# Weight units in two halves, a deeper last prep, staged mixer weights and four smaller edits in an eight-core decoder block

## The chip, the cores and the metric

The kernel runs on one Trainium2 chip, on all 8 cores at once; each core works alone on 2048 of the 16384 tokens. The metric is the device time of one execution in microseconds (us), taken from the slowest core. The cores are two dies of four. In some executions one die (sometimes both) is granted a lower TensorE clock, and the time is 2 to 18% longer. Such an execution is called slow here; the others are fast. Because many executions were slow on one die only, I also use **die medians**: the median span of the four cores of a die, for those dies on which every core was granted at least 0.98 of full clock. Their intervals are 1.96 standard errors over the dies, so with 5 to 8 dies they are a little too narrow. Several kernels of one job share the chip and the executions of the kernel before.

## The reference, cut to what matters

```python
def swiglu_ffn(h, w_in, w_out):                      # D_MODEL 2048, D_FF 5632
    gate, up = jnp.split(h @ w_in, 2, axis=-1)
    return (jax.nn.silu(gate) * up) @ w_out
# mixer_block: z = h @ w_in + b_in; a pooling branch and a convolution branch
#   conv branch: GLU -> causal depthwise conv (31 taps) -> LayerNorm over channels -> silu -> @ conv_w_proj
#   merged by gates, then @ w_out                                         [cut]
def reference(x, ...):                               # 4 x 4096 tokens, float32
    x = x + 0.5 * swiglu_ffn(rmsnorm(x, ffn1_norm), ffn1_w_in, ffn1_w_out)
    x = x + mixer_block(rmsnorm(x, mix_norm), ...)
    x = x + 0.5 * swiglu_ffn(rmsnorm(x, ffn2_norm), ffn2_w_in, ffn2_w_out)
    return rmsnorm(x, final_norm)
```

## The kernel before

A core keeps its tokens as rows of 128 channels by tokens, and handles them as two halves of about 1024 tokens. The order of stages is the whole plan of the kernel: FFN 1 on the first half (**A**), the mixer's first part on that half, FFN 1 on the second half (**B**), the mixer's second part on the first half and its first part on the second half, FFN 2 on one half (**C**), in which the mixer's last part ("mixer 2b") is inserted after the first unit of in 2, and FFN 2 on the other half (**D**). Each FFN pass has three chunks of the hidden width, each with an input product ("in 0" to "in 2") and an output product ("out 0" to "out 2").

The FFN products use seven products per 2x2 block of weights in place of eight. A weight unit holds four blocks; two of the seven products use a block as it is ("raw"), five use sums of blocks that VectorE makes. One transfer brings the unit, and every reader waits for the whole of it:

```python
    def send(self, key):
        ...
        bufs = self.half[h:h + size]
        if name in self.staged:                       # already stored as f16: SyncE's queue
            self.P.op(SP, lambda e: e.dma_start(out=dst, in_=src), reads=[self.staged[name][idx]], writes=bufs, ...)
        else:                                         # cast f32 -> f16: GpSimd's queue
            self.P.op(POOL, lambda e: e.dma_start(out=dst, in_=src), reads=self.after.get(len(self.units), ()),
                      writes=bufs, ...)

    PRODUCTS = ((("raw", 0), 3), (("raw", 3), 2), (("d", 0), 6), (("rs", 1), 0), (("rs", 0), 1), (("es", 0), 4),
                (("es", 1), 5))

    def make_sums(ws, sm, nk, part):                  # on VectorE
        rb = ws.bufs
        if part == 0:
            vt(c2(L), sm.d[:, 0:L], rq[:, 0, :], rq[:, 3, :], ALU.add, rb, [sm.b[2]])
        ...
```

Three pieces of background work run in between on VectorE, ScalarE and the queues, one small step after each product. `landed(t0, us)` delays the next step until an estimated time after `t0`; it is a pause in the program's order, not a wait on the chip.

```python
    def prep_forms(nm, h, cg, forms, tiles=None):     # last prep: X2 rows -> normalised inputs of D, two rows deep
        ...
        def load(k):
            if k < 8:
                pair_load(nm, h, k, tiles)
                sent[k] = state["pe"]
            if k - 1 in sent:
                landed(sent[k - 1])

        def done(j):                                  # one conv channel block is finished: store it, CC is reused next
            dma(dr["CD"][S, j], CC.t, [CC.b], [b_CD[S][j]], CC.sem)
            ...
                parts = square_add(CC.t, CC.b, g.t[:, 0:TB], g.b) + [lambda: leave(g)]

            def inverses():                           # LayerNorm: 1/std of all tokens, one instruction
                vec(TB * 6 / 960.0, lambda e: e.reciprocal(out=LNT[:], in_=LNT[:]), [b_LNT], [b_LNT])

        def put(j):                                   # second LayerNorm: one row of CN, one buffer for all rows
                act(CNT.t, t, AF.Silu, ...)           # ScalarE writes the row ...
                dma(dr["CN"][:, j, :], CNT.t, [CNT.b], [b_CND[j]], CNT.sem)   # ... and it is stored
```

The first weights wait for row 4 of x, and the second half of x waits for the first weights (`W.after = {0: b_X0[0, 4], ...}` and `ahead = ... W.units[0].bufs`). The mixer's weights (conv_w_proj, w_out) come as f32 with a cast in both mixers.

## Time and profile before

| | kernel before |
|---|---|
| first three executions | 4760.07, 4757.5 us (fast), 5540.49 us (slow) |
| die medians, 34 dies of the first three jobs of experiments | 4742.5 us (95%: +-2.0) |

In a timeline each line is: start, us, engine, line of the source, operation, out<-in, count, and in brackets how long the engine had stood and which engine or transfer ended that. BIG stands for all of the program's large on-chip rows; raw is the buffer of the weight units; CC is the row of one conv channel block, CD and CN are its copies off the chip, before and after the second LayerNorm; MD is what the mixer's last part reads, and X2 what FFN 2 reads. The timeline of core 1 before, around the conv block whose CC buffer is written again:

```profile
1818.68 0.81 DVE L1049 TENSOR_SCALAR BIG<-BIG,CST 128x1024 f32<-128x1024 f32 x1 [5.78 <-DMA CD<-BIG]
...
1823.41 7.08 PE L555 MATMUL PSUM<-BIG 128*128 128x512 bf16 x32 [1.54 <-DVE BIG L477]
...
1836.88 2.75 PE L555 MATMUL PSUM<-BIG,raw 128*128 128x512 bf16 x12 [3.80 <-DVE BIG L477]
```

VectorE stands 5.78 us until the store of CC to CD has landed. TensorE pays twice: 1.54 us at once, and 3.80 us thirteen microseconds later, when VectorE is the releaser again.

**A ledger by stage.** Sums of waits say little about where time goes, so I cut each core's span at the evictions from PSUM to PSUM that ScalarE makes twice in every group of seven products (680 in each trace, in all kernels). A stage ends at the second eviction of its last group. I use it for all kernels below; values are medians over undisturbed cores of the profiled execution (in after_again, best2 and neither, single cores at 0.983 are left out). Single executions of one kernel differ by up to 7 us in stages that are limited by transfers (B out 0, C in 1, C out 1, C in 2), the whole of A by 5 us, and by less than 1 us in most others.

### The profile page before, as it was taken

The numbers are of one execution on the slowest core, as the hardware profiler recorded it, in microseconds if no ns is written. First come the engines' busy times: TensorE is split into PE (matmuls) and PEld (weight loads), VectorE is DVE, ScalarE is ACT, GpSimd is POOL, SyncE is SP. The second block draws the span as 40 slices with busy tenths as digits, with TensorE's granted clock in tenths as the row PEclk, the third lists the DMA queues.
The fourth block names the chain that finished last, engine by engine and source line by source line (L and its number), as shares of the span: only waits on it lengthen the run. The fifth ranks groups of instructions, "written<-read, shape, count | busy, mean of one in ns | idle before, by whom it ended". The sixth has DMA issues, their size and how long they took to land.

```text
span 4929.9 us, 68574 instructions; the slowest of 8 cores (4715.5 to 4929.9 us)
## 1 busy us (share of the span) xinstructions
PE 4777.7 (97%) x24626; PEld 2483.7 (50%) x24626; DVE 3469.9 (70%) x3829; ACT 1425.1 (29%) x2157; POOL 287.0 (6%) x484
## 2 busy tenths in 40 slices
PE   6999999999999999999999999999999999999996
PEld 4878888765444444444444444444444444444442
DVE  7767577778778788656878788876555566565567
ACT  4333333522112222334320112223202223232232
POOL 0000100000000000000000000000100000000000
PEclk9999999999999999999999999999999989999998
DMA  7887887687668777977657875484986495766854
GB/s 147 127 215 117 149 131 135 198 187 157 119 117 125 213 134 144 159 137 201 142 115 185 199 170 105 99 151 104 191 222 135 110 195 104 154 114 146 161 133 175
DMA packets 177468, 742.23 MB, mean 151 GB/s; under 512 B 18160, under 2 KB 19312, under 8 KB 148976
## 3 DMA queue, kind: packets, MB, share of 16 engines
q0 software_dynamic: 71552, 383.02, 49.0%
q1 hardware_dynamic: 105584, 354.83, 22.2%
q8 instruction: 203, 3.33, 0.3%
q14 instruction: 129, 1.06, 0.1%
HBM read 899.39 MB, written 208.54 MB: 225 GB/s over the span
## 4 chain that ended last, share of the span: by engine, by line
PE 89%; DMA 4%; DVE 4%; issue 2%; ACT 1%; SPq 0%; DVEq 0%; ACTq 0%; POOLq 0%; POOL 0%
PE PSUM L555 89%; DMA raw<-ffn_w_in 2%; DVE BIG L477 2%; DVE BIG L480 1%; ACT BIG L490 1%; PE PSUM L567 1%; DMA BIG<-MD 1%; DMA raw<-ffn_o 0%; ACT PSUM L490 0%; DMA BIG<-X2B 0%; DMA BIG<-xA 0%; DMA LNT<-xA 0%; SPq L496 0%; DVE RSA L584 0%; DVE RSB L584 0%
## 5 line engine op out<-in xcount | busy, mean ns | idle before, releaser
L555 PE MATMUL PSUM<-BIG 128*128 128x512 bf16 (+1 forms) x13200 | 2504.5, 352 | 41.4 <-ACT PSUM L490 25.1
L555 PE MATMUL PSUM<-BIG,raw 128*128 128x512 bf16 (+2 forms) x11368 | 2352.6, 368 | 71.4 <-DMA raw<-ffn_w_in 38.2
L555 PEld LDWEIGHTS PSUM<-BIG 128*128 128x128 f16 x13200 | 1327.4, 101 | 1175.3 <-issue 389.7
L555 PEld LDWEIGHTS PSUM<-BIG,raw 128*128 128x128 f16 x11368 | 1144.5, 101 | 1220.3 <-issue 406.8
L477 DVE TENSOR_TENSOR BIG<-BIG 128x1024 f32<-128x1024 f32 (+11 forms) x958 | 741.2, 801 | 662.1 <-ACT BIG L490 616.2
L477 DVE TENSOR_TENSOR BIG<-raw 128x2048 f16<-128x2048 f16 (+3 forms) x816 | 827.0, 1015 | 348.2 <-PE PSUM L555 223.6
L490 ACT ACTIVATE PSUM<-PSUM 128x512 f32<-128x512 f32 (+1 forms) x680 | 339.4, 499 | 1480.9 <-PE PSUM L555 1467.9
L490 ACT ACTIVATE BIG<-PSUM 128x512 f32<-128x512 f32 (+3 forms) x684 | 468.8, 685 | 853.7 <-PE PSUM L555 843.4
L480 DVE SCALAR_TENSOR_TENSOR BIG<-BIG,CST 128x1024 f32<-128x1024 f32 (+2 forms) x520 | 638.9, 1232 | 28.8 <-DVE BIG L477 6.8
L477 DVE TENSOR_TENSOR BIG<-PSUM,BIG 128x1024 f32<-128x1024 f32 (+3 forms) x532 | 476.1, 896 | 129.8 <-PE PSUM L555 106.2
L490 ACT ACTIVATE BIG<-BIG 128x1024 f32<-128x1024 f32 (+2 forms) x386 | 337.4, 906 | 412.1 <-DVE BIG L477 381.6
L490 ACT ACTIVATE BIG<-BIG,CST 128x512 f32<-128x512 f32 (+4 forms) x287 | 212.6, 752 | 637.0 <-DVE BIG L477 624.7
L480 DVE SCALAR_TENSOR_TENSOR BIG<-BIG 128x1024 bf16<-128x1024 f32 (+2 forms) x236 | 241.9, 1026 | 2.3
L211 POOL DMA_DIRECT2D raw<-ffn_w_in x176 | 104.0, 603 | 2094.4 <-DVE BIG L477 916.4
L477 DVE TENSOR_TENSOR BIG<-PSUM,RSA 128x352 f32<-128x352 f32 (+1 forms) x136 | 81.0, 599 | 71.1 <-PE PSUM L555 69.2
L477 DVE TENSOR_TENSOR BIG<-PSUM,RSB 128x512 f32<-128x512 f32 x112 | 76.8, 689 | 73.2 <-PE PSUM L555 72.8
L477 DVE TENSOR_TENSOR BIG<-BIG,RSA 128x1056 f32<-128x1056 f32 (+1 forms) x96 | 118.2, 1250 | 12.2 <-DMA BIG<-CD 9.9
L211 POOL DMA_DIRECT2D raw<-w_in x112 | 59.5, 531 | 950.5 <-PE PSUM L555 928.7
L477 DVE TENSOR_TENSOR RSB<-RSB,BIG 128x1024 f32<-128x1024 f32 x66 | 80.7, 1223 | 46.4 <-ACT BIG L490 45.3
L477 DVE TENSOR_TENSOR RSA<-RSA,BIG 128x528 f32<-128x528 f32 (+1 forms) x95 | 86.0, 906 | 15.4 <-ACT BIG L490 13.2
L490 ACT ACT_TABLE_LOAD x38 | 48.8, 1283 | 75.5 <-DVE BIG L477 59.5
L480 DVE SCALAR_TENSOR_TENSOR BIG<-BIG,CST,RSB 128x512 bf16<-128x512 f32 (+1 forms) x80 | 64.3, 853 | 7.9 <-DMA BIG<-X2B 6.8
(64 smaller groups left out, 414.5 us busy)
## 6 DMA issues: line engine op xcount, KB each, us to landing
raw<-ffn_w_in POOLq DMA_DIRECT2D x176, 1024.0 KB, 10.9
raw<-ffn_o SPq DMA_DIRECT2D x64, 896.0 KB, 8.2
raw<-w_in POOLq DMA_DIRECT2D x112, 512.0 KB, 7.0
raw<-ffn_o SPq DMA_DIRECT2D x32, 1024.0 KB, 7.2
ffn_o<-ffn_w_out POOLq DMA_DIRECT2D x32, 896.0 KB, 17.6
BIG<-xB SPq DMA_DIRECT2D x24, 1024.0 KB, 9.6
X2A<-BIG POOLq DMA_DIRECT2D x24, 1024.0 KB, 12.8
X1A<-BIG SPq DMA_DIRECT2D x32, 528.0 KB, 6.9
```

The costliest lines, as they stand in the source:

```text
L211: self.P.op(POOL, lambda e: e.dma_start(out=dst, in_=src), reads=self.after.get(len(self.units), ()), writes=bufs, semkey=self.semk[POOL][ ...
L477: vec(cost, lambda e: e.tensor_tensor(out=out, in0=in0, in1=in1, op=op), reads, writes)
L480: vec(cost, lambda e: e.scalar_tensor_tensor(out=out, in0=in0, scalar=scalar, in1=in1, op0=op0, op1=op1), reads, writes)
L490: P.op(ACT, lambda e: e.activation(out=out, in_=in_, func=func, **kw), reads=reads, writes=writes)
L555: ins = e.matmul(d, a, r, start=(start and i == 0), stop=(stop and i == last), skip_group_check=True)
L567: P.op(PE, lambda e: e.matmul(bk(bank, w), ONES[:], rhs, start=start, stop=stop), reads=rbufs + [b_ONES], writes=[b_bank[bank]])
```

## The change

The intent is to shorten the waits of TensorE that the profile names, and its cold starts. The core of the diff, part by part (cut where "..."; unchanged lines left out):

```diff
 # 1. units as two transfers; blocks reordered so that the first half holds both raw blocks
-            self.P.op(POOL, lambda e: e.dma_start(out=dst, in_=src), reads=self.after.get(len(self.units), ()), ...)
+            eng, reads = POOL, reads if reads and isinstance(reads[0], list) else [reads] * size
+        n //= size
+        for i in range(size):
+            self.P.op(eng, lambda e, i=i: e.dma_start(out=dst[:, i * n:(i + 1) * n], in_=src[:, i * n:(i + 1) * n]),
+                      reads=reads[i], writes=bufs[i:i + 1], semkey=self.semk[eng][h + i], incval=16)
-    PRODUCTS = ((("raw", 0), 3), (("raw", 3), 2), (("d", 0), 6), ...
+    PRODUCTS = ((("raw", 0), 3), (("raw", 1), 2), (("d", 0), 6), ...
-                    A, rb = rawv[:, a, :], ws.bufs
+                    A, rb = rawv[:, a, :], ws.bufs[0:1]
 # 2. the last prep three rows deep, its first rows asked for before C in 2
+    def prep_last(cg, forms):
+        tiles = [own[0], [(LNT[:], b_LNT, s_x0[15]), (RS[0][:, 0:TB], b_RS[0], s_x0[16])], own[1]]
+        ...
+        def after(k):
+            load(k + 3)
+            if k < 7:
+                landed(sent[k + 1], 16.0)
 # 3. the reciprocal in two halves
-            def inverses():
-                vec(TB * 6 / 960.0, lambda e: e.reciprocal(out=LNT[:], in_=LNT[:]), [b_LNT], [b_LNT])
+            def inverses(s):
+                half = LNT[:, s * 512:(s + 1) * 512]
+                vec(512 * 6 / 960.0, lambda e: e.reciprocal(out=half, in_=half), [b_LNT], [b_LNT])
+                idle(3.0)
 # 4. a pause before CC is written again
+            t0 = state["pe"]
-                parts = ... + [lambda: leave(g)]
+                parts = ... + [lambda: (leave(g), landed(t0, 18.0))]
 # 5. the mixer's second pass reads f16 copies that the FFN's spare time staged
+                     + [("conv16", "conv_w_proj", i) for i in range(8)] + [("out16", "w_out", i) for i in range(8)])
-            ws = W.get("conv_w_proj", cb)
+            ws = W.get("conv16" if S else "conv_w_proj", cb)
-            ws = W.get("w_out", j)
+            ws = W.get("out16" if S and j < 8 else "w_out", j)
 # 6. the start: first weights asked for by rows 0 and 6, norm factors on ScalarE, constant matmuls
-            W.after = {0: b_X0[0, 4], 1: b_X0[1, 4], 2: [b_LNT, b_RS[1]]}
+            W.after = {0: [b_X0[0, 0], b_X0[0, 6]], 1: b_X0[1, 4], 2: [b_LNT, b_RS[1]]}
+        if p == 1:
+            act(v[:, 1:6:4, :], xb[:, ::-1, :], AF.Copy, [bb, b_CST], [b[0], b[2]], scale=cst(C_N1 + k + 8))
+            make_forms(HFA, k, p)
+            return
+    warm(170)
 # 7. the end: constant matmuls ahead of the last column sums
+    warm(48)
```

## The prediction

> **What bounds the kernel now.** I read the span and clock of every core first. The profiled execution is a slow one: die 1 has a lower clock. The two undisturbed timed runs are 4757.5 and 4760.07 us, so I read core 1, the slowest core of the undisturbed die, and count from 4759 us.
>
> ```profile
> core 1: 4739.6 us, clock 0.987
> core 6: 4929.9 us, clock 0.936
> die 0 (median of its cores): 4728.6 us, clock 0.988
> die 1 (median of its cores): 4901.2 us, clock 0.943
> ```
>
> Next the page of core 1: TensorE is busy 4538.1 of 4739.6 us, VectorE 3459.6, ScalarE 1425.7, GpSimd 286.8. TensorE is the bound, so only two things can be gained: the 201 us in which it waits, and the time in which it runs at half clock after a wait. In the table of 100 us windows, the stretches without waits hold 465 matmuls of 512 columns each (215 ns a matmul) or 891 of 264 columns (112 ns). At those rates all the bf16 matmuls of the list of forms (8100 + 7920 of 512, 7396 of 264, 1152 of 352 columns at an interpolated 149 ns) take 3444 + 830 + 172 = 4446 us. So about 290 us of the span is loss, and the first 28 and last 40 us are a large part of it that nobody can remove wholly.
>
> Third, TensorE's waits by releaser, core 1:
>
> ```profile
> PE PSUM L555 <- DVE BIG L477: 62.4, 49, 7.7
> PE PSUM L555 <- DMA raw<-ffn_w_in: 61.6, 14, 27.9
> PE PSUM L555 <- ACT PSUM L490: 26.6, 37, 3.7
> ```
>
> The columns are us in all, times, longest. Fourth, the timeline at those waits (start, us, what, then the idle time before it and who ended it):
>
> ```profile
> 27.95 4.12 PE L555 MATMUL PSUM<-BIG,raw 128*128 128x264 bf16 x18 [27.95 <-DMA raw<-ffn_w_in]
> ...
> 3242.57 6.55 DVE L1135 RECIPROCAL LNT<-LNT 128x1024 f32<-128x1024 f32 x1
> ...
> 3251.58 3.67 PE L555 MATMUL PSUM<-BIG 128*128 128x512 bf16 x9 [4.37 <-DVE BIG L477]
> ...
> 3404.26 5.64 PE L555 MATMUL PSUM<-BIG,raw 128*128 128x512 bf16 x16 [5.80 <-DMA raw<-ffn_w_in]
> ...
> 3838.23 2.93 DVE L480 SCALAR_TENSOR_TENSOR BIG<-BIG,CST,RSB 128x512 bf16<-128x512 f32 x4 [6.85 <-DMA BIG<-X2B]
> ...
> 3843.68 9.53 PE L555 MATMUL PSUM<-BIG 128*128 128x512 bf16 x32 [7.68 <-DVE BIG L477]
> ```
>
> Each names one target of the change: the late first weights; the long reciprocal that holds VectorE in front of a PSUM eviction; a weight unit that lands late; and the last prep, whose row lands late and holds VectorE in front of the weight sums that TensorE needs.
>
> **What the Trainium skill says.** "TensorE: Matmul & The Clock Gate", Part 1: the array runs at 1.2 GHz until it has been busy about 3.4 us and falls back after about as long an idle window. The trace agrees: 16 matmuls take 3.61 us normally, but 5.64 us after the 5.80 us wait above; and the granted clock reads 0.50 in the sparse stretch 44 to 52 us. "DMA: Bandwidth & Descriptors", section "SWDGE vs HWDGE vs iDMA": a cast needs GpSimd's queue, which is why only weights already stored as f16 can go by SyncE. Section "Issuing engines are not separate DMA queues" of the same page: all issuers share the 16 engines. The trace shows what the kinds cost: GpSimd's queue 50.4% of 4739.6 us for 383 MB, 6.2 us per MB of all 16 engines; SyncE's 23.4% for 355 MB, 3.1 us per MB.
>
> **The change, part by part.**
>
> *Units as two transfers.* The four blocks of a unit are reordered so that the first half holds both blocks that the raw products (and the sum d) read; the second half is needed only by the later sums. The same bytes move; 176 GpSimd and 96 SyncE transfers become twice as many. At 531 ns for a half-size issue (the w_in row) against 602 ns, GpSimd gains some 80 us of work, 6% to 8% of its span, which hides. A unit lands 10.5 us (median) after its issue, and 16 to 31 us at the chunk borders, where it shares the engines with accumulating stores. The data time of a unit is 1.05 MB x 6.2 = 6.5 us at best, so the first half should land 3.3 to 6 us ahead of the whole. The 13 waits for ffn_w_in after the start add up to 61.6 - 27.9 = 33.7 us (5.80, 5.63, 4.64, 4.39, 3.61 and eight under 2). The raw and d products take 3.45 + 1.7 us before a sum of the second half is used, and that sum takes 1.22 us on VectorE; so a remainder of about 1 us stays in the long ones. Five of them are followed by a cold start of 1.6 to 2.0 us. Gross 33.7 - 6 + 9 = 36 us; but those stretches have a DMA share of 0.95 to 0.99, so TensorE running sooner asks for the next unit sooner. I choose three quarters: **27 us**.
>
> *Last prep three rows deep.* It takes away the 7.68 us wait and its cold start: 32 matmuls took 9.53 us against 6.9 at 215 ns, 2.6 us. Some of the neighbouring VectorE wait (2.1 us for X2B at 3823) goes too, but it cost TensorE nothing. 10.3 us, of which I count **9**, as the rows compete with the same weight traffic.
>
> *The reciprocal in two halves.* There are two of 6.55 us; only the one at 3242 stops TensorE: 4.37 us plus 5.18 - 3.61 = 1.6 us cold. **5 us**.
>
> *A pause before CC is written again.* VectorE waited 5.78 us for the CD store at 1818, TensorE 1.54 us after it: **1.5 us**.
>
> *Start.* The first weights are now asked for when the first row has landed (about 9 us instead of 16.4) and wait for no later row; the squares of row 4 no longer wait for the unit (ScalarE stood 8.77 us until 27.84, and forms 6 and 7 were made only after it). But the squares of row 0 now wait for the first half, and the second half of x still has to arrive: its last row lands at 48.2 us, with DMA shares of 0.9 to 1.0 in 10 to 48 us. So TensorE's first product starts some 8 us sooner, yet most of that runs into the x rows. From 50 to 130 us VectorE is the bound (windows: busy 7.98 + 24.45 + 36.72 = 69.2 of 80 us); eight tensor_scalars of 0.49 us leave it for ScalarE, which has room (5.51 + 18.03 + 14.32 of the same 80 us): 4 us. Rows earlier by 2 to 3 us, 1 to 2 us of cold time saved: **8 us**. The 170 constant matmuls themselves (some 20 us at 213 ns cold, then 107) end before x is there; they block nothing, but warmth is lost again in the sparse stretch up to 48 us, so I give them almost nothing.
>
> *End.* At 4700.54 TensorE starts the four f32 column sums at half clock, and the second is evicted at 4706.75. The 48 constant matmuls run from 4696.4 for about 48 x 107 ns = 5.1 us, 1 us past the moment the sums could start, then four sums at 0.85 us instead of 1.7 at first: **1.7 us**.
>
> *Mixer weights staged.* 16 more cast copies (0.52 MB each, 3.3 us of all engines, 52 us in all) are spread over the third FFN; in the second mixer 16 loads go from 6.2 to 3.1 us per MB, 26 us of engine time less, where TensorE after 3404 waits for nothing. Net with the extra completions: **-3 us**.
>
> Sum 27 + 9 + 5 + 1.5 + 8 + 1.7 - 3 = 49 us: 4759 - 49 = **4710 us**, about 1.0% faster.
>
> **Rivals.** (a) *The waits move instead of going*: the border stretches are limited by DMA bandwidth, so a unit that starts sooner makes the next one late; for it, shares of 0.95 and up; against it, the stretches right after them fall to 0.4 to 0.6 and the shortage is a burst. Then part one gives 10 us and the time is about 4728. (b) *VectorE takes over*: it is busy 73%, and in 50 to 130 us 87%; sums that start sooner queue behind the same conv taps. It would eat some 10 to 15 us: about 4722. (c) *The cold time is larger than I count*: 100 us windows with clocks of 0.97 to 0.98 are many, the 1.3% missing from the mean of 0.987 is 62 us of span, and every wait pushed under 3.4 us takes back its cold start; with a fuller gain at the start it would be 80 us or more: about 4675. (d) *Staging and doubled transfers cost*: more stores in 2850 to 3350, where the share is already 0.89 to 0.95 in places; 10 us lost, 4720.
>
> **Range and chances.** (a), (b) and (d) together give 4745, (c) 4672; the range is **4672 to 4745**. Faster by over 2% needs 95 us, a third of all loss including ends that mostly stay: 0.07. Slower by over 2% would need a new wait that nothing here shows: 0.01. Within 2%: 0.92.
>
> **What would show it.** On an undisturbed core after: waits for ffn_w_in outside the start under 10 us in all, and no 5 us group of 16 raw matmuls at the chunk borders; no wait near 3843 over 3 us; no 4 us wait after the reciprocal; the first real product near 20 us but the dense stretch that follows reached only some 8 us sooner than before; the end 1 to 2 us shorter. The prediction is wrong if waits of VectorE or of SyncE's queue grow by what the weights' waits lose, or if the start alone gives 20 us or more.

## The result, and the profile after

All ratios are the mean time of one kernel's fast executions over the mean of the other's fast ones of the same rounds, so not quite the ratio of medians. The changed kernel's three fast executions were 4699.34, 4714.33 and 4720.19 us (mean 4711.3), the fast ones of before beside them 4757.5, 4760.07 and 4765.06 us (mean 4760.9): ratio **0.9896**, 95% interval 0.9857 to 0.9934. Other executions were slow (up to 5519.87 and 5540.49 us) and are left out. By die medians it is 4693.8 us (+-3.9, 14 dies, with the repeat below) against 4742.5: **49 us less**. These 14 dies leave out two executions (4714.33 and 5519.87 us); with them it is 4694.6 (16 dies), 48 us less, and every difference to 4693.8 below shrinks or grows by 0.8. The prediction was 4710 us, 49 less. The sum was right; most of its terms were not, and the experiments are about that.

The profiled execution was fast on both dies. From the view of all cores, after:

```profile
die 0 (median of its cores): 4689.3 us, clock 0.990
die 1 (median of its cores): 4691.4 us, clock 0.990
```

The busy times of the engines on core 1 after (engine, busy us, share of the span, instructions):

```profile
PE 4543.9 (97%) x24844; PEld 2429.9 (52%) x24844; DVE 3458.1 (74%) x3823; ACT 1428.0 (30%) x2165; POOL 379.9 (8%) x660
```

GpSimd went from 286.8 to 379.9 us, as expected and hidden. TensorE's busy time is nearly unchanged, but 25.6 us of it are now the constant matmuls: the real products take 20 us less (fewer of them run cold), and the time outside busy went from 201.5 us to 138.8, 25.6 of the difference filled with constants. 19.8 + 62.7 - 25.6 is the 57 us by which this core is shorter. TensorE's waits by releaser on core 1 after:

```profile
PE PSUM L560 <- ACT PSUM L495: 42.3, 35, 16.8
...
PE PSUM L560 <- DVE BIG L482: 36.5, 43, 4.0
...
PE PSUM L560 <- DMA raw<-ffn_w_in: 9.9, 3, 4.8
```

Read against the three lines of before: the weights went from 61.6 us (33.7 without the start) to 9.9, VectorE from 62.4 to 36.5 with its longest wait down from 7.7 to 4.0. But the first line went **up**, from 26.6 to 42.3, and its longest wait is 16.8 us where it was 3.7. The timeline of core 1 after, at that wait:

```profile
3310.82 0.32 SPq L501 DMA_DIRECT2D CN<-BIG  x1
...
3334.38 1.24 ACT L495 ACTIVATE BIG<-BIG,CST 128x1024 bf16<-128x1024 f32 x1 [19.86 <-DMA CN<-BIG]
...
3336.24 8.98 PE L560 MATMUL PSUM<-BIG 128*128 128x512 bf16 x34 [16.80 <-ACT PSUM L495]
```

A row of CN is sent at 3310.82 and lands some 23 us later; ScalarE must write the next row into the same buffer, stands 19.86 us, and cannot empty PSUM meanwhile; TensorE stands 16.80 us and is cold after it (the granted clock averages 0.54 from 3330 to 3340 us). Nothing like this is in the trace before, and the longest such wait is 9 to 17 us on all eight cores. The eight CN stores of this core land in 2.3 to 23.5 us, with a median of 4.3 (before: 2.3 to 12.4); the slow one met a stretch with the transfers' share at 1.0.

The reciprocals are two of 3.35 us, and TensorE's longest wait near them is 1.17 us instead of 4.37 (timeline of core 1 after):

```profile
3229.20 3.35 DVE L1187 RECIPROCAL LNT<-LNT 128x512 f32<-128x512 f32 x1
...
3235.01 3.61 PE L560 MATMUL PSUM<-BIG 128*128 128x512 bf16 x16 [1.17 <-ACT BIG L495]
```

The start, core 1 before. The three lines are the first weights' issue, the squares that wait for them, and the last row of x, which lands at 48.2:

```profile
16.38 0.67 POOL L211 DMA_DIRECT2D raw<-ffn_w_in  x1 [15.69 <-DMA BIG<-xA]
...
27.84 1.18 ACT L490 ACTIVATE BIG<-BIG 128x528 f32<-128x528 f32 x2 [8.77 <-DMA raw<-ffn_w_in]
...
48.23 0.49 DVE L1538 TENSOR_SCALAR BIG<-RSB,CST 128x528 bf16<-128x528 f32 x1 [0.56 <-DMA RSB<-xA]
```

and after:

```profile
1.48 20.16 PE L583 MATMUL PSUM<-ONES 128*128 128x256 bf16 x170 [1.48 <-DVE ONES L1563]
...
8.69 0.67 POOL L214 DMA_DIRECT2D raw<-ffn_w_in  x1 [7.99 <-DMA BIG<-xA]
...
19.65 1.18 ACT L495 ACTIVATE BIG<-BIG 128x528 f32<-128x528 f32 x2 [8.57 <-DMA raw<-ffn_w_in]
...
21.47 1.06 PE L560 MATMUL PSUM<-BIG,raw 128*128 128x264 bf16 x8
...
22.70 0.53 POOL L214 DMA_DIRECT2D raw<-ffn_w_in  x1 [13.35 <-DMA BIG<-xA]
...
46.62 1.05 POOL L214 DMA_DIRECT2D raw<-ffn_w_in  x2 [5.27 <-DMA RSB<-xA]
```

TensorE's first real product starts at 21.5 instead of 27.95 us. But ScalarE still stands 8.57 us for the weights, the second half of the unit is asked for only at 22.70, the second half of x waits for it, and the last row of x lands at 46.6 instead of 48.2 us. From 25 to 40 us the granted clock is 0.50, so the warmth of the 170 constant matmuls is gone before there is work. They even stand in its way: the first real product follows their end without a gap, while without them (run old_prep, cores 4 and 5) it starts at 18.4 and 19.4 us.

The ledger, us per stage (medians of the profiled execution; stages that differ by less than 1 us are left out, and so are C out 0, 88.5 to 87.4, and the mixer's first part before B, 478.8 to 480.5). The rows add up to 42 us, not 49: the profiled execution of before was a short one (4728.6 us on its undisturbed die, against 4742.5 for all 34).

| stage | before | after | after, repeated | difference of the first two |
|---|---|---|---|---|
| start, first two units | 68.3 | 67.9 | 67.9 | -0.4 |
| B out 0 | 97.8 | 90.1 | 97.0 | -7.7 (one execution each; within scatter) |
| B out 1 | 95.2 | 88.5 | 88.5 | -6.7 |
| B in 2 | 205.0 | 198.9 | 199.8 | -6.1 |
| C in 1 | 180.1 | 173.1 | 174.4 | -7.0 |
| C out 1 | 88.6 | 101.8 | 100.5 | **+13.2** |
| C in 2, first unit | 34.2 | 30.0 | 29.8 | -4.2 |
| mixer 2b | 178.7 | 175.2 | 176.0 | -3.5 |
| C out 2 | 105.5 | 98.3 | 98.3 | -7.2 |
| D in 0 | 176.5 | 169.2 | 169.2 | -7.3 |
| D in 1 | 174.3 | 171.4 | 171.9 | -2.9 |
| last unit and end | 62.4 | 60.5 | 60.2 | -1.9 |

### The profile page after: what moved, and what is told of

It reads as the page before. It is cut to its first block, busy times and chain, and to the rows that moved or that the text cites.

```text
span 4697.8 us, 69578 instructions; the slowest of 8 cores (4681.5 to 4697.8 us)
## 1 busy us (share of the span) xinstructions
PE 4536.1 (97%) x24518; PEld 2432.6 (52%) x24844; DVE 3457.4 (74%) x3823; ACT 1428.1 (30%) x2165; POOL 380.0 (8%) x660
## 4 chain that ended last, share of the span: by engine, by line
PE 84%; DVE 5%; DMA 5%; issue 3%; ACT 1%; SPq 0%; DVEq 0%; ACTq 0%; POOL 0%; POOLq 0%
PE PSUM L560 84%; DVE BIG L482 3%; DMA raw<-ffn_w_in 2%; DVE BIG L485 1%; DMA raw<-ffn_o 1%; ACT BIG L495 1%; PE PSUM L572 0%; DMA CN<-BIG 0%; DMA BIG<-X1B 0%; ACT PSUM L495 0%; DMA BIG<-xA 0%; DVE RSB L482 0%; DMA RSB<-xA 0%; DVE RSA L601 0%; DVE RSA L482 0%
## 5 line engine op out<-in xcount | busy, mean ns | idle before, releaser
L560 PE MATMUL PSUM<-BIG 128*128 128x512 bf16 (+1 forms) x13040 | 2368.6, 339 | 67.7 <-ACT PSUM L495 38.7
L560 PE MATMUL PSUM<-BIG,raw 128*128 128x512 bf16 (+2 forms) x11202 | 2218.3, 354 | 53.5 <-DVE BIG L482 29.5
L560 PEld LDWEIGHTS PSUM<-BIG 128*128 128x128 f16 x13200 | 1286.6, 98 | 1104.8 <-issue 97.0
L560 PEld LDWEIGHTS PSUM<-BIG,raw 128*128 128x128 f16 x11368 | 1112.6, 98 | 1106.5 <-issue 68.8
L482 DVE TENSOR_TENSOR BIG<-raw 128x2048 f16<-128x2048 f16 (+3 forms) x816 | 825.6, 1014 | 294.3 <-PE PSUM L560 175.8
L495 ACT ACTIVATE BIG<-PSUM 128x1024 f32<-128x1024 f32 (+3 forms) x684 | 468.5, 685 | 770.1 <-PE PSUM L560 766.2
L214 POOL DMA_DIRECT2D raw<-ffn_w_in x352 | 197.8, 606 | 1870.9 <-DVE BIG L482 1086.8
L482 DVE TENSOR_TENSOR RSB<-RSB,BIG 128x1024 f32<-128x1024 f32 x66 | 80.7, 1222 | 38.8 <-ACT BIG L495 37.7
L914 POOL DMA_DIRECT2D X2A<-BIG x24 | 26.1, 1085 | 398.9 <-DVE BIG L482 279.9
## 6 DMA issues: line engine op xcount, KB each, us to landing
ffn_o<-ffn_w_out POOLq DMA_DIRECT2D x32, 896.0 KB, 18.4
X2A<-BIG POOLq DMA_DIRECT2D x24, 1024.0 KB, 15.3
```

What stands on the lines that cost most here:

```text
L214: self.P.op(eng, lambda e, i=i: e.dma_start(out=dst[:, i * n:(i + 1) * n], in_=src[:, i * n:(i + 1) * n]), reads=reads[i], writes=bufs[i:i ...
L482: vec(cost, lambda e: e.tensor_tensor(out=out, in0=in0, in1=in1, op=op), reads, writes)
L495: P.op(ACT, lambda e: e.activation(out=out, in_=in_, func=func, **kw), reads=reads, writes=writes)
L560: ins = e.matmul(d, a, r, start=(start and i == 0), stop=(stop and i == last), skip_group_check=True)
L914: P.op(POOL, lambda e: e.dma_start(out=ap, in_=t.rows(), accum_op=ALU.add), reads=t.b, writes=db, semkey=t.sem2, incval=16)
```

## The experiments

Twelve runs were made, all with correct results. Most undo one part of the changed kernel. The table gives the die medians (95% over dies) and the ratios to before where enough fast executions allowed one. Line numbers in the profiles of experiments differ by a few from those of the changed kernel, as the sources differ.

| run | edit | die median us (dies) | ratio to before |
|---|---|---|---|
| before | | 4742.5 +-2.0 (34) | |
| after, both runs | | 4693.8 +-3.9 (14) | 0.9896; again 0.9889 [0.9772, 1.0005] |
| one_transfer | part 1 undone | 4709.1 +-4.0 (7) | 0.9924 [0.9901, 0.9946] |
| old_prep | parts 2 and 7 and the 170 constants undone | 4709.3 +-3.0 (6) | 0.9992 [0.9875, 1.0108] |
| whole_recip | part 3 and the ScalarE factors undone | 4710.9 +-3.0 (5) | none |
| no_pause | part 4 undone | 4706.1 +-3.6 (6) | 0.9940 [0.9881, 0.9999] |
| no_stage | part 5 undone | 4708.6 +-2.9 (5) | none |
| two_cn | two CN buffers added | 4692.8 +-2.8 (6) | 0.9919 [0.9876, 0.9962] |
| pause_b | pause only in B | 4693.7 +-2.9 (6) | none |
| best | pause_b and a mended start | 4689.8 +-3.4 (6) | 0.9872 [0.9823, 0.9921] |
| best2 | best and two CN buffers | 4687.4 +-2.7 (12) | 0.9859 [0.9800, 0.9919] |
| neither | parts 1 and 2 undone | 4719.1 (2) | none |
| split_only | before with part 1 alone | 4737.6 +-8.8 (7) | none |

### Is it the two transfers? (one_transfer)

```diff
-        n //= size
-        for i in range(size):
-            self.P.op(eng, ... dst[:, i * n:(i + 1) * n] ..., writes=bufs[i:i + 1], ...)
+        self.P.op(eng, lambda e: e.dma_start(out=dst, in_=src), reads=reads[-1], writes=bufs, ...)
-            W.after = {0: [b_X0[0, 0], b_X0[0, 6]], ...
+            W.after = {0: b_X0[0, 4], ...
```

> The changed kernel with each weight unit again as one transfer and one semaphore (the new order of the blocks stays; the first unit again waits for row 4). Stage times are medians over undisturbed cores; A, B, C, D are the four FFN half passes, 'in' and 'out' their chunks' two products. Theory 1, the split is what removed the weight waits at the chunk borders: the stages fall back to those of the kernel before, B out 0 from 91 to 97 us, B out 1 from 88.5 to 95, B in 2 from 198 to 205, C in 2 first from 30 to 34, D in 0 from 169 to 173 (its weight wait only), D in 1 from 171 to 174; 25 to 30 us in all, about 4737 us. Rival, the stalls went because the order of the work on GpSimd's and SyncE's queues changed with the other parts: those stages stay within 2 us and the time at about 4712 us.

The die median rose by 15 us (4709.1 against 4693.8), not by 27. The weights' waits came back at once. TensorE's wait for weights on core 1 of this run, then one of them in its timeline:

```profile
PE PSUM L558 <- DMA raw<-ffn_w_in: 27.8, 13, 5.4
```

```profile
4131.45 5.30 PE L558 MATMUL PSUM<-BIG,raw 128*128 128x512 bf16 x16 [2.06 <-DMA raw<-ffn_w_in]
```

The line shows the cold start that the prediction counted: 16 matmuls in 5.30 us instead of 3.61, after a wait of 2.06. So undoing the split adds about 18 us of waits on core 1 (9.9 to 27.8; 5.4 of them are the first unit's, which this run also asks for later) and cold time with them; over the eight cores the waits are 27 to 36 us in this run and 10 to 15 after. By stage it is worth 3.1 us in B in 2, 2.6 in C in 1, 2.5 in C in 2, 1.9 in D in 0, 4.6 in D in 1 and 1.9 in D in 2; B out 0 read 99.5, which one execution of the changed kernel nearly reached too (97.0). B out 1 stayed at 88.5, so that gain has another cause (the pause, below). The mechanism of the prediction holds; its size does not.

### What is the split worth alone? (split_only)

The kernel before with part 1 of the diff and nothing else, except that the first weights are asked for by rows 0 and 6:

```diff
 # against the changed kernel (cut: the rows of the old prep, the list of staged copies)
-    begin, prep_rest = prep_last(C_N3, FX)
-    bg.extend(begin)
-    prep_rest()
+    prep_forms("X2", 1, C_N3, FX, ROWX)
-    (lambda: inverses(1), lambda: inverses(0), roots, ...
+    (inverses, roots, ...
-    [lambda: (leave(g), landed(t0, 18.0))]
+    [lambda: leave(g)]
-    W.get("conv16" if S else "conv_w_proj", cb), W.get("out16" if S and j < 8 else "w_out", j)
+    W.get("conv_w_proj", cb), W.get("w_out", j)
-        if p == 1:                                # norm factors on ScalarE
-            ...
-    warm(170), warm(48)
```

> The kernel before with the first part alone: weight units as two transfers (and the first weights asked for by row); prep, reciprocal, pause, start, end and staging as before. Undone alone, this part cost 15 us of the die median (4709.1 against 4693.8); the prediction counted 27. If its worth does not depend on the other parts: 4742 - 15 = 4727 us die median, ratio 0.9965 to 0.9975. If the prediction's 27 was right and the other parts hide some of it: 4715 us, ratio 0.994 to 0.995. Stage readings: the first input chunk of the last half should lose its 7 us (169 to 171 us instead of 176.5), the second output chunk of the second half stay near 95 or 96 us (no pause), the third output chunk of the third half near 106 to 109, that is with the old prep's wait.

Its dies average 4737.6 us (+-8.8; six of the seven between 4730 and 4738) against 4744.9 in the same job: 7 us less, with an interval that also holds 0 and 15. Its start read 71.8 us against 68.3, as asking for the weights by rows came without ScalarE's help, so the split itself is worth some 3.5 more: an estimate of 11. All but one execution were slow on some die, and the profiled one had 4 cores at a clock of 0.963 to 0.971, so its stages are read only where they repeat. On cores 4 to 7 (0.983 to 0.988) the expected readings are B out 1 at 96.2 and C out 2 at 110.2, as expected, and D in 0 at 172.7, where 169 to 171 was expected. One pair does, on all eight cores: C in 2's first unit was 23 to 31 us and mixer 2b 181 to 190. Adding the two for each core shows what happens there:

| run (cores) | first unit of C in 2 | mixer 2b | sum per core |
|---|---|---|---|
| before (0 to 3) | 29.3 to 37.7 | 175.2 to 179.4 | 208.7 to 215.8 |
| split_only (0 to 7) | 23.3 to 30.5 | 181.4 to 190.2 | 210.9 to 215.3 |
| no_stage (0 to 7) | 24.1 to 30.5 | 181.2 to 190.4 | 211.7 to 215.7 |
| after (0 to 7) | 27.9 to 30.7 | 175.2 to 177.3 | 205.0 to 205.9 |

Where the unit came sooner, the mixer that follows it waited longer, by the same amount. This is the prediction's rival (a), waits that move instead of going, in a place it had not named: without staged mixer weights the split gains nothing here.

### The staging (no_stage)

```diff
-            ws = W.get("conv16" if S else "conv_w_proj", cb)
+            ws = W.get("conv_w_proj", cb)
-            ws = W.get("out16" if S and j < 8 else "w_out", j)
+            ws = W.get("w_out", j)
-                     + [("conv16", "conv_w_proj", i) for i in range(8)] + [("out16", "w_out", i) for i in range(8)])
+                     )
```

> The changed kernel with all mixer weights read as f32 by GpSimd's queue, nothing of them staged. Predicted was a cost of 3 us for the staging, so the span would fall by up to 3 us. The stages tell where: if the second mixer's shorter time in the changed kernel (178.7 to 175.2 us) and the gain of C in 2 first (34.2 to 30.0) or D in 0 (176.5 to 169.2) came from the lighter loads, they go back by 2 us or more; if they came from the split units or the prep, they stay within 1 us. C in 0 and C in 1, which carry the copies, fall by up to 1 us.

Mixer 2b went from 175.2 to 186.1 us, and above the 178.7 of before. The timeline of core 1 of this run:

```profile
3403.79 19.15 PE L559 MATMUL PSUM<-BIG,raw 128*128 128x512 bf16 x88 [1.58 <-DMA raw<-conv_w_proj]
...
3422.79 0.69 DVE L481 TENSOR_TENSOR BIG<-BIG 128x512 bf16<-128x512 f32 x1 [3.80 <-DMA BIG<-MD]
...
3424.23 1.89 PE L559 MATMUL PSUM<-BIG,raw 128*128 128x512 bf16 x8 [1.28 <-DVE BIG L481]
...
3431.66 148.61 PE L559 MATMUL PSUM<-BIG,raw 128*128 128x512 bf16 x680 [2.51 <-DVE BIG L481]
```

TensorE waits once for the conv weights, and then several times for VectorE, which waits for rows of MD that share the engines with the f32 weights. In the changed kernel TensorE has no wait at all in this stage on core 1. The prediction gave staging a cost of 3 us because the trace before showed no wait there; once the units land sooner there is one, and staging is worth 9 us in this stage and the unit ahead of it (213.9 to 205.2, the medians of the sums), 15 by die medians.

### The last prep and the constant matmuls (old_prep)

```diff
-    ROWX = [[Row(f"rowx{i}{a}", lo + 4096 * a, TB) for a in range(2)] for i, lo in enumerate((CV0, XB0 + 50176))]
+    ROWX = [Row(f"rowx{i}", lo, TB, F32, 2) for i, lo in enumerate((XB0 + 50176, CV0))]
-    begin, prep_rest = prep_last(C_N3, FX)
-    bg.extend(begin)
-    prep_rest()
+    prep_forms("X2", 1, C_N3, FX, ROWX)
-    warm(170)
-    warm(48)
```

> The changed kernel with the last prep two rows deep as before, and without both stretches of constant matmuls. Theory: C out 2 goes from 98.3 back to 105 us (the wait of 7.7 us and its cold start), D in 0 stays within 3 us of 169.2 if its gain came from the split weights, or goes back to 176 if it came from the prep. Without the constant matmuls the end (last output row block and normalisation) goes from 60.5 to 62.2 us, and the start stays at 68 us, because the clock is lost again before the dense stretch; the rival for the start says that the warm clock pays there: 70 us or more.

Die 0 of the profiled execution was disturbed (0.974 to 0.982), so cores 4 to 7 are read. C out 2 went from 98.3 to 109.4 us (105.9 to 112.5 by core), and the old wait with its cold start was back (timeline of core 5 of this run):

```profile
3825.64 9.60 PE L560 MATMUL PSUM<-BIG 128*128 128x512 bf16 x32 [6.51 <-DVE BIG L482]
```

So undoing the deeper prep costs 11 us there; between before and after the stage gained 7.2 (105.5 to 98.3). The prediction took 10.3 and counted 9. The end went from 60.5 to 62.2 us, 1.7 as predicted for the 48 constants (in the changed kernel they take 5.40 us, and each group of four f32 sums after them 1.88 us, where before the groups took 3.75 and 2.56). The start read 67.8 against 67.9: the 170 constants are worth nothing that can be seen. D in 0 stayed at 170.3, so the prep alone does not explain its gain.

### Neither the split nor the deeper prep (neither)

The edits of one_transfer and of old_prep together, except that both calls of `warm` stay:

```diff
-            self.P.op(eng, ... dst[:, i * n:(i + 1) * n] ..., writes=bufs[i:i + 1], ...)
+        self.P.op(eng, lambda e: e.dma_start(out=dst, in_=src), reads=reads[-1], writes=bufs, ...)
-    begin, prep_rest = prep_last(C_N3, FX)
-    bg.extend(begin)
-    prep_rest()
+    prep_forms("X2", 1, C_N3, FX, ROWX)
```

> The changed kernel with units as one transfer again and the last prep two rows deep again, the only two parts of which each was undone alone without the first input chunk of the last FFN half going back from 169.2 to 176.5 us. If either of the two suffices there: 175 to 177 us now. Rival (the gain comes from another part, the staging's or the pause's shift of the second mixer): 169 to 172 us still. The third output chunk of the third FFN half should read 109 us, the second of the second 88.5.

D in 0 had fallen from 176.5 to 169.2 us and neither undoing alone brought it back (171.1 and 170.3). With both undone it is 176.5 again on the median of six undisturbed cores, to the tenth the value of before. The timeline of core 1 of the kernel before, then of this run, at the wait behind it:

```profile
3882.73 5.30 PE L555 MATMUL PSUM<-BIG,raw 128*128 128x512 bf16 x16 [4.64 <-DMA raw<-ffn_w_in]
```

```profile
3842.38 5.98 PE L558 MATMUL PSUM<-BIG,raw 128*128 128x512 bf16 x16 [4.45 <-DMA raw<-ffn_w_in]
```

One late unit, 4.5 us and 1.7 to 2.4 of cold start. Either of the two parts suffices to remove it, so its 7 us belong to neither alone. C out 2 read 102.6, less than the 109 expected.

### The reciprocal in halves, and the norm factors (whole_recip)

```diff
-            def inverses(s):
-                half = LNT[:, s * 512:(s + 1) * 512]
-                vec(512 * 6 / 960.0, lambda e: e.reciprocal(out=half, in_=half), [b_LNT], [b_LNT])
-                idle(3.0)
+            def inverses():
+                vec(TB * 6 / 960.0, lambda e: e.reciprocal(out=LNT[:], in_=LNT[:]), [b_LNT], [b_LNT])
-        if p == 1:                                # norm factors on ScalarE
-            act(v[:, 1:6:4, :], xb[:, ::-1, :], AF.Copy, ...)
-            make_forms(HFA, k, p)
-            return
```

> The changed kernel with the LayerNorm reciprocal in one instruction again, with no pause after it, and with the second half's norm factors back on VectorE at the start. Theory for C in 1: the 4.4 us wait and its cold start come back, 173 to 179 us. For the new wait of 9 to 17 us in C out 1 (ScalarE waits for the store of CN): if the pauses of the split reciprocal pushed the LayerNorm into that stage, it shrinks by half or more, 100.7 to 94 us or less; if the pause after the store of CD or the doubled transfers did it, it stays at 98 us or more. Start: 68 us either way if the x rows and not VectorE set it, which is what I now think; 72 us if VectorE's 4 us counted, as predicted.

Cores 4 to 7 are read (die 0 was at 0.976 to 0.982). C in 1 went from 173.1 to 180.1 us, exactly the value of before, and B in 2 from 198.9 to 203.4. The timeline of core 5 of this run repeats the lines of before to a hundredth:

```profile
3238.42 6.54 DVE L1186 RECIPROCAL LNT<-LNT 128x1024 f32<-128x1024 f32 x1
...
3247.43 5.14 PE L560 MATMUL PSUM<-BIG 128*128 128x512 bf16 x16 [4.37 <-DVE BIG L482]
```

So the two halves are worth about 7 us in C and 4.5 in B; the prediction had 5, and had said that only the one in C stops TensorE. In the trace before that is so: within 14 us of the first long reciprocal TensorE has no wait over 0.4 us on cores 0 to 3. In this run one of 4.4 to 4.7 us follows it on each of cores 4 to 7. Core 5:

```profile
2032.49 6.54 DVE L1186 RECIPROCAL LNT<-LNT 128x1024 f32<-128x1024 f32 x1
...
2041.50 5.30 PE L560 MATMUL PSUM<-BIG 128*128 128x512 bf16 x16 [4.37 <-DVE BIG L482]
```

So in B the halves take away a wait that the kernel before did not have and that other parts of the change would have brought; which part moves the reciprocal there is not shown (in split_only it stops nothing). C out 1 stayed at 99.6 (one core read 88.0), so the halves are not what causes the new wait. The start went up by 3.4 us, which is what the offload to ScalarE is worth, close to its predicted 4; as the start as a whole gained only 0.4, the rest of part 6 costs about as much as this gains.

### The new wait: one CN buffer, or the pause? (two_cn, no_pause, pause_b)

My theory after reading the result: the pause of part 4 costs time in the queue of background steps, so the second LayerNorm's rows come later. By the order in which the two programs issue their instructions, the first of the eight CN rows comes after the 240th group of seven products instead of the 238th, the last after the 248th instead of the 245th; C out 1 is groups 240 to 247. All of them now fall among the accumulating stores of C out 1, where the transfers' share is near 1, and one CN store takes 23.5 us; before, six of the eight fell there, and the longest took 12.4. The rival: one buffer for CN is simply too few whenever units come sooner, whatever the pause does.

First the buffer (two_cn):

```diff
+    CNU = Row("cnu", YB0 + 50176, TB, BF16)
-                act(CNT.t, t, AF.Silu, ...)
-                dma(dr["CN"][:, j, :], CNT.t, [CNT.b], [b_CND[j]], CNT.sem)
+                c = (CNT, CNU)[j % 2]
+                act(c.t, t, AF.Silu, ...)
+                dma(dr["CN"][:, j, :], c.t, [c.b], [b_CND[j]], c.sem)
```

> The changed kernel with two buffers in turn for the CN rows of the second LayerNorm, so that ScalarE's next row need not wait for the store of the row before. If that store is the whole cause of the new wait, C out 1 goes from 100.7 to 88 us as in the kernel before, and the time from 4710 to about 4698 us; if the stage is short of DMA bandwidth as such, the wait moves to the CD loads or to the weights of that stage and C out 1 and C in 2 together lose less than 4 us.

C out 1 went from 101.8 to 93.8 us, only part of the way to 88.6. The wait for the CN store is gone, and the load of the next CD row has taken its place (timeline of core 1 of this run):

```profile
3346.49 1.23 DVE L483 TENSOR_TENSOR BIG<-BIG,RSB 128x1024 f32<-128x1024 f32 x1 [8.32 <-DMA BIG<-CD]
...
3351.44 5.80 PE L561 MATMUL PSUM<-BIG 128*128 128x512 bf16 x14 [9.83 <-DVE BIG L483]
```

So the store was not the only thing too slow: the loads of these rows are slow in that stretch too. Then the pause (no_pause):

```diff
-                parts = square_add(...) + [lambda: (leave(g), landed(t0, 18.0))]
+                parts = square_add(...) + [lambda: leave(g)]
```

> The changed kernel without the wait of 18 us of model time after each store of CD, in both LayerNorms. The second LayerNorm's rows stand in the program two to three output blocks earlier then, where the kernel before has them (put at blocks 238 to 245, against 240 to 248). Theory: the pause pushed them into C out 1, whose accumulating stores fill the DMA engines, and that is the new wait: C out 1 goes from 101.8 to 88 to 91 us. In return B out 1 goes from 88.5 back to about 95 us, because VectorE again waits for the store of CD there. Rival, the doubled transfers or the staging make CN's store slow: C out 1 stays above 97 us.

Cores 0 to 3 are read (die 1 was at 0.974 to 0.982). C out 1 is back at 88.5 us (87.6, 87.7, 89.4 and, on core 2, 98.1), and on core 1 TensorE's longest wait for ScalarE's evictions at 3.7: the pause is a cause of the new wait, shown. The single buffer is the other: on cores 0, 2 and 3 ScalarE still waits 2.6 to 10.5 us for a CN store. In B the price is as clear; the timeline of core 1 of this run:

```profile
1811.60 0.81 DVE L1099 TENSOR_SCALAR BIG<-BIG,CST 128x1024 f32<-128x1024 f32 x1 [8.07 <-DMA CD<-BIG]
...
1816.34 8.75 PE L560 MATMUL PSUM<-BIG 128*128 128x512 bf16 x32 [3.83 <-ACT BIG L495]
...
1829.80 4.87 PE L560 MATMUL PSUM<-BIG,raw 128*128 128x512 bf16 x14 [2.13 <-DVE BIG L482]
```

B out 1 is 96.2 us against 88.5 with the pause, and B in 2 is 203.2 against 198.5 in the next run, which differs from this one by the pause in B only. So the pause is worth 7.7 + 4.7 = 12.4 us in B; the prediction said 1.5. The die medians of the two runs differ by 12.4 (+-4.6) as well (4706.1 and 4693.7). That next run (pause_b):

```diff
-                parts = square_add(...) + [lambda: (leave(g), landed(t0, 18.0))]
+                parts = square_add(...) + [lambda: (leave(g), S or landed(t0, 18.0))]
```

> The changed kernel with that pause only in the first LayerNorm's pass (B), not in the second's (C). By the theory it has both gains: B out 1 stays at 88.5 us and C out 1 falls from 101.8 to 88 to 91 us, about 11 us off the span, to some 4700 us timed. If the two stages are tied in another way, one of them stays where the changed kernel or the kernel before has it.

B out 1 keeps its 88.5 us. C out 1 is 93.8 (87.5 to 96.8 by core), better than 101.8 but not the 88 to 91 I had expected, and C in 1 is 175.8 where the changed kernel has 173.1 and 174.4. The die median, 4693.7, is that of the changed kernel. What is saved in C out 1 is largely spent in stages around it. What is left in C out 1 is the wait for the CN store itself: on seven of the eight cores ScalarE's longest is 5.1 to 10.3 us. Core 6 of this run:

```profile
3330.61 1.24 ACT L495 ACTIVATE BIG<-BIG,CST 128x1024 bf16<-128x1024 f32 x1 [10.32 <-DMA CN<-BIG]
...
3332.48 7.85 PE L560 MATMUL PSUM<-BIG 128*128 128x512 bf16 x26 [7.26 <-ACT PSUM L495]
```

So the rival, that one buffer is too few, is partly right: without the pause the wait is shorter, not gone.

### A better version (best, after_again, best2)

The run best is pause_b with a mended start. The mended start: GpSimd waits for the row itself before each half of the unit without counting as its reader, the second half is asked for after row 4 (two rows sooner), and the second half of x waits for the first half of the unit only.

```diff
+            if eng == POOL and reads[i]:
+                self.P.wait_for(POOL, reads[i])
+                reads[i] = ()
-            W.after = {0: [b_X0[0, 0], b_X0[0, 6]], ...
+            W.after = {0: [b_X0[0, 0], b_X0[0, 4]], ...
-            ahead = ... if k < 2 else W.units[0].bufs
+            ahead = ... if k < 2 else W.units[0].bufs[0:1]
```

> The kernel with the pause only in B, and a mended start: GpSimd waits for the rows that only set the pace of the first weight transfers without being counted as a reader of them, so ScalarE's squares of row 0 need not wait for the first half unit (8.45 us on core 4 of the changed kernel); the second half goes after row 4 instead of row 6; the second half of x waits for the first half unit alone. Theory: the start is set by the landing of the last x row (47 us), for which the DMA engines stood half idle at 20 to 25 us; so the first stage falls from 67.9 to 62 to 65 us. Rival: it is set by VectorE's forms and sums, and stays at 67 us or more. Together about 4695 us timed, faster than both kernels.

The start fell to 66.9 us by median (64.6 to 69.0), less than expected; C out 1 was 89.9. The ratio, 0.9872, is below the changed kernel's 0.9896, but the intervals overlap. So the changed kernel was run again beside a version with both cures of the new wait.

The run after_again is the changed kernel without an edit.

> The changed kernel once more, unedited, beside the next one on the same chip. Expected: the same ratio to the kernel before as at first, 0.987 to 0.992; the stretches that no DMA limits as before (98.3 us in the third output chunk of the third FFN half, 88.5 us in the second of the second), and the new wait on the CN store again (over 100 us in the second output chunk of the third FFN half).

The run best2 is best with the two CN rows of two_cn (the same edit as shown there).

> The changed kernel with the pause only in the first half, two rows in turn for CN, and the start edit of the run best. My theory (the CN store holds ScalarE because the second LayerNorm's last rows run into the accumulating stores): both cures together leave no wait on CN or CD in the second output chunk of the third FFN half: 88 to 90 us there instead of 101.8, and a ratio to the changed kernel of the same rounds of 0.996 to 0.998 (13 us there and 1 at the start, less 0 to 3 lost elsewhere). Rival (the stretch is limited by DMA bandwidth, so what is not waited for there is waited for in the next stretches): the same ratio as the changed kernel, within 0.002.

The repeat gave the same picture: 0.9889, C out 1 at 100.5, C out 2 at 98.3, B out 1 at 88.5. The class of this repeat is "unclear", as its interval holds 1. In best2 C out 1 is 90.0 us and the start 65.0; no core waits for a CN store in that stage. TensorE's waits on core 0 of best2:

```profile
PE PSUM L564 <- DVE BIG L486: 38.3, 40, 4.6
...
PE PSUM L564 <- ACT PSUM L499: 28.7, 37, 4.0
...
PE PSUM L564 <- DMA raw<-ffn_w_in: 8.9, 4, 3.5
```

No wait of these three kinds is longer than 4.6 us, and ScalarE's line is back near the 26.6 of before. best2 has the lowest die median, 4687.4 us (12 dies), 6.4 (+-4.7) less than the changed kernel and 55 less than before. As a ratio to the changed kernel that is 0.9986 by die medians, and 0.9970 by the ratios of the same rounds (0.9859 / 0.9889), whose intervals are too wide to tell it. Theory (0.996 to 0.998) and rival (within 0.002) each have one measure on their side. The ledger says why it is less than the 12 us of the cured stage and 3 of the start: C in 1 went up to 177.5 and C out 0 by 1.1. The rival is partly right: part of the time in C belongs to a stretch that is short of bandwidth, and moves when one wait is removed. In C out 1 itself VectorE now waits up to 12.3 us for the FFN's output weights (core 2), where after the change it waited 2.7 at most. best2 beats both kernels; over the changed one it does so by little.

## Why the prediction was right in sum and wrong in its terms

| term | predicted us | measured us | by which run |
|---|---|---|---|
| two transfers | 27 | 15 undone; 7 +-10 alone (11 without its start) | one_transfer, split_only |
| last prep | 9 | 11 undone; 7 before to after | old_prep, C out 2 |
| reciprocal | 5 | 7 in C; 4.5 in B, undone only | whole_recip |
| pause before CC | 1.5 | 12.4 in B, -13 in C out 1 | no_pause, pause_b |
| start | 8 | 0.4 | ledger before and after |
| end | 1.7 | 1.7 | old_prep |
| staging | -3 | 9 in its stages, 15 by die median | no_stage |

- **The bound.** Right: TensorE is still the bound, and the change touched only its waits. VectorE did not take over (rival b): its busy time is the same and TensorE waits less for it. GpSimd's extra work (rival d) is hidden.
- **Two transfers.** Step and mechanism right, size wrong. The waits outside the start fell from 33.7 to 9.9 us on core 1, within the "under 10" that the prediction asked for (this holds on four of the eight cores; the other four have 11.2 to 15.3), and the cold starts were there to be won. What failed is the factor of three quarters: core 1 was the core with the most of these waits on its die (the others had 23 to 26 us outside the start), and where the stretch stays short of bandwidth the next stage gives the gain back (first unit of C in 2 and mixer 2b, above). A unit that still comes late after the change (a group of 16 raw matmuls with 5.30 us behind 4.77 at 3372.87 on core 1) falsifies the line "no 5 us group of 16 raw matmuls".
- **Last prep.** Right within 2 us either way.
- **Reciprocal.** "Only the one at 3242 stops TensorE" was a right reading of the kernel before, and C in 1 gained 7.0 us for the 5 predicted. What it could not see is that in the changed kernel the first one would stop TensorE as well (4.37 us in whole_recip).
- **Pause.** The step that failed is "TensorE 1.54 us after it". The 3.80 us wait that follows in the same timeline goes with it (with the pause B out 1 is 88.5 us and neither wait is there), and the other half of the pause, in C, brought a wait of 9 to 17 us. The prediction's test, "wrong if waits of VectorE or of SyncE's queue grow by what the weights' waits lose", pointed the right way but at the wrong engine: it was ScalarE, behind a store.
- **Start.** "Rows earlier by 2 to 3 us" and "4 us" for the offload were added up. The rows came 1.6 us earlier on core 1, the second half of the unit was asked for later than the whole had been, and ScalarE's wait for the weights (8.77 us) was not removed but moved forward (8.57), as row 0's squares count as waiting for the row's reader, the weights' transfer. Had I checked who waits for the second half of the unit, the 8 would have been smaller. Wrong too, though without a cost that shows, is that the constant matmuls "block nothing": the first real product waits for their end.
- **Staging.** The step "where TensorE after 3404 waits for nothing" took the trace before as fixed. It was true of core 1 before, probably because its unit came late (37.5 us for the first unit of C in 2) and gave the mixer's loads a head start; core 0, with a unit as late (37.7), still spent 178.0 us in the mixer, so this reason is not shown.
- **The sum.** Too much for the split and the start (+20), too little for reciprocal, prep and staging (about -20), and in the pause +11 in B against -13 in C. These errors cancel; the total of 49 us is luck as far as the terms go. The balance is rough, as values from undone kernels overlap (next paragraph).
- **The range.** Its ends are not quite its own sums: (a), (b) and (d) together are 4710 + 18 + 12 + 10 = 4750, not 4745, and (c) is about 4675 in one place and 4672 in the next. Nothing hangs on it here.

**What stays open.** Undone one at a time, the five larger parts cost 15.3 + 15.5 + 17.1 + 14.8 + 12.3 = 75 us by die medians, more than the whole gain of 49. Staging and split depend on each other, as shown. In B in 2 three undone parts cost 3.1 + 4.5 + 4.7 = 12.3 us where the change gained 6.1, as the first reciprocal stops TensorE in the changed program and not before. C out 1 improves a little in most of the undone kernels. I have not accounted for all of it.

## What to carry to other kernels

A wait that a trace does not show can be hidden by the very wait you remove: ask what the engine will need next, and whether those transfers were using the time. An inserted pause moves everything behind it in the same queue of work; check in which stretch the later steps, with their own stores and single buffers, will then land. And when a prediction's total is right, undo the parts one by one before you trust its terms.

## What the Trainium skill lacked or had wrong

- "DMA: Bandwidth & Descriptors", "Anatomy of one DMA", gives about 2 us plus bytes over 436 GB/s for one transfer (its fit is for GpSimd's path). For a CN row of 256 KB, sent by SyncE, that would be an estimated 2.6 us. In the trace after three of the eight stores took 2.3 to 2.5 us, but the longest took 23.5, and half units of 448 KB took 24.5 us (median of four) in the stretch from 3290 to 3340 us, where the transfers' share is near 1. I found no figure there for one transfer among many on the same engines.
- The same page, "SWDGE vs HWDGE vs iDMA", says that only GpSimd's queue casts, and the traces agree. It gives no price: here GpSimd's queue, which carries the cast loads and the accumulating stores, took 6.2 us of all 16 engines per MB, SyncE's plain transfers 3.1. The cast's own share was not separated.
- "TensorE: Matmul & The Clock Gate", Part 1, says that three or more cores of a die in dense matmuls bring the whole die to 13/16 of the clock, to be budgeted for. Clocks of 0.81 to 0.82 do appear (5546.26 and 5564.16 us), but 34 dies of the kernel before, with all four cores dense, ran at 0.98 or more. Slow dies with a mean in between (0.86 to 0.96) were at 13/16 for a part of the time: on core 6 of the trace before (mean 0.936) the granted clock was 0.8125 for 1471 us, 1.0 for 3345 and 0.5 for 83, and nothing else. So the state is there, but it comes and goes; what sets it off was not found.
- The same part puts the fall back to the cold clock after an idle window of about 3.4 us. (A later section of the page tells of short idle gaps that are enough when they are frequent, without a length.) Here shorter gaps were enough when little stood between them: after the 170 constants ended at 21.6 us, TensorE ran pairs of matmuls of 0.60 us with gaps of 2.3 to 2.5 us, and the granted clock read 0.50 from 25 to 40 us.
